# The mixers' first group in a one-core macaron block: where its loads, its first sums and the norms' squares stand

## The chip, the cores and the metric

The kernel runs on one core of a Trainium2 chip. The metric is the device time of one execution in microseconds (us), the median of several runs. Five engines work side by side, each through its own list of instructions in order, and wait for each other by semaphores: TensorE (PE, with its weight loads shown apart as PEld), VectorE (DVE), ScalarE (ACT), GpSimd (POOL) and SyncE (SP). SP, POOL and ACT also issue DMAs, each on a queue of its own.

## The reference

One block of a streaming encoder on 256 tokens of width 2048, all in float32: a half-step SwiGLU network, then attention and retention side by side on one wide projection, then a second half-step network and a last norm.

```python
x = x + 0.5 * swiglu_ffn(rmsnorm(x, norm_ffn1_g[l]), ...)
h = rmsnorm(x, norm_mix_g[l])
proj = h @ w_in[l]
q_a, k_a, v_a, q_r, k_r, v_r, g_r, gate_a, gate_r = jnp.split(proj, IN_SPLIT_POINTS, axis=-1)
...
x = x + merged @ w_out[l]
x = x + 0.5 * swiglu_ffn(rmsnorm(x, norm_ffn2_g[l]), ...)
return rmsnorm(x, norm_final_g)
```

`rmsnorm` multiplies a row by the reciprocal root of its mean square and by a gain per channel. The kernel multiplies by the gain ahead of the products and by the root (`rstd`) behind them.

## The kernel before

**Numbers in two halves.** Each float32 weight tile is split into a high part `hi`, a cast on ACT (L134), and a low part `lo`, a subtraction on DVE (L135). The left operands are split in the same way (L456, L457). A product is then three matmuls: high with high (L145), low left with high (L146), high left with low (L148). PE takes the weight's low part last, so `lo` may be ready a little later than `hi`.

**Entries.** The program is one list, `steps`, of entries. A standard entry multiplies two 128-row pieces of a 512-column block for both token halves, 12 matmuls; its weights come in one 512 KB tile `raw`, loaded by SP into a ring of five (`RAW_BUFS`). An entry of a `Strassen` group has 6 matmuls. A group computes two 512-column blocks at once by Strassen's scheme, over four weight pairs `k0`, `x0` to `k3`, `x3`, which POOL loads into act tiles (L552). Its first sum, `x += k` on DVE (L541, in `first`), gives the weights of the entries marked `s`; entries marked `r` use `k` alone. Groups are named by the entry at which they begin: `z390` is the mixers' first, `queries`. The low part of its entry `s` with pair 2 is `loz39002s`.

**What sets the order.** `run` (L254 on) goes through the entries. At entry c it first prepares entries up to c+3 (`prep_upto`: cast, subtraction, and what else `prep` does), then runs what `later(n, fn)` has put down for c, then issues c's matmuls. `load_some` lets a group's loads into the program from a given entry on, one an entry; for the first group of a `weave` that begins at eight entries ahead of the last one laid down (`first`, L722), for z390 at entry 382. In a group the first sum is part of `prep`, of the `r` entry of the same pair.

**The seam between the first network and the mixers.** Entries 376 to 383 are the last pass of the first network's down projection, four 512-column blocks of two entries each. When a block ends, `down_done` adds the product to x (L682, DVE, two pieces `xall`), and `done` of `x_updated` squares the new x with a row sum (L436, ACT, `nmsq`), at once, and three entries later calls `norm.put`: eight transposes on PE into two side banks (L468, `nmp`), four scalings on ACT out of these banks (L473, `nmx`), and the split `nma` (L456, L457). After the last square DVE adds up the sums and POOL takes the root (`tot` L442, `v` L382, `nmrstd` L383), and DVE makes `nmminus` from it (L445). There are two side banks. Entries 384 to 389 are the first six of the mixers' first projection, and at 390 z390 begins, woven with further standard entries (394, 399, 402). Four more operands of the norm (`nms5` to `nms7`, `nms3`) are made on DVE and ACT for the group's sums, from `nmf` (L494 to L503, L507, L508). The same `x_updated` stands between the mixers and the second network, with the norm `n2` and the group `z704`.

Of the kernel before, what the change touches and what calls it, by code (L numbers as in the profile page):

```python
# [18 lines left out]
D = 2048  # L19
# [7 lines left out]
NB = 512  # L27
# [7 lines left out]
EXTRA = 2  # L35
# [5 lines left out]
MIX_LEAD = 6  # L41
RET_WAIT = (14, 5)
HELD = 6
MIX_ADDED = (0,)
HEAD_AT = (3, 6, 10, 13, 17, 20, 24, 27)

MIX_SHARE = (0.5,) * 4 + (1.0,) * 4 + (0.0,) * 4 + (0.2,) * 4
SHARE = (0.75,) * 4 + (1.0,) * 4 + (0.0,) * 4 + (0.2,) * 4
ADDED = (0, 1)
ADD_WAIT = 6  # L50
# [30 lines left out]
def block_kernel(ctx: ExitStack, tc: tile.TileContext, x, g1, w1g, w1u, w1d, gm, w_in, rel, woa, wor, wo,  # L81
# [25 lines left out]
    steps = []  # L107
# [6 lines left out]
    def later(n, fn):  # L114
        due.setdefault(state["step"] + n, []).append(fn)
# [408 lines left out]
    class Strassen:  # L524
# [3 lines left out]

        def __init__(self, norm, w1, col1, w2, col2, evict, added=()):
            self.added, self.summed = added, set()  # L530
            self.add_wait = ADD_WAIT
            self.norm, self.w, self.col, self.evict = norm, (w1, w2), (col1, col2), evict
            self.x, self.kept, self.acc, self.wide = {}, {}, {}, {}
            self.name = f"z{len(steps)}"

        def rows(self, side, jc):
            j = KC * jc
            return ((2 * (j // 4) + side) * 4 + j % 4) * P

        def first(self, jc):  # L540
            nc.vector.tensor_add(self.x[jc], self.x[jc], self.kept[jc])  # L541
# [5 lines left out]
        def loads(self):  # L547


            def go(tiles, i, jc):  # L550
                tiles[jc] = apool.tile([P, KC, NB], F32, tag="act", name=f"{self.name}{'kx'[i]}{jc}")
                nc.gpsimd.dma_start(tiles[jc], chunk(self.w[i], self.rows(0, jc), self.col[i]))  # L552

            def add_on(jc):
                if jc not in self.summed:
                    self.summed.add(jc)
                    nc.gpsimd.dma_start(self.x[jc], self.kept[jc], accum_op=ALU.add)

            def second(jc):
                go(self.x, 1, jc)  # L560
                if jc in self.added:
                    later(self.add_wait, lambda: add_on(jc))

            return [
                (lambda jc=jc: second(jc)) if i else (lambda jc=jc: go(self.kept, 0, jc))
                for jc in range(HALF_K // KC) for i in range(2)
            ]
# [12 lines left out]
        def step(self, phase, jc, of_sum):  # L580
            made = {}
            name = f"{self.name}{phase}{jc}{'rs'[of_sum]}"
            n = HALF_K // KC

            def load():
                made["raw"] = weights_tile(f"raw{name}")
                i = 2 - phase
                fetch(made["raw"], self.w[i], self.rows(1, jc), self.col[i])

            def third():  # L590

                x, k = self.x[jc], self.kept[jc]
                nc.vector.tensor_sub(k, x, k)
                nc.gpsimd.dma_start(x, chunk(self.w[0], self.rows(1, jc), self.col[0]), accum_op=ALU.add)

            def prep():
                x = self.x[jc]
                if not of_sum:
                    if phase == 0:
                        made["w"] = split(self.kept[jc], name)  # L600
                        if jc not in self.added:
                            self.summed.add(jc)
                            self.first(jc)
                        return
                    raw = made.pop("raw")
                    made["w"] = split(raw, name)
                    if phase == 1:
                        nc.vector.tensor_add(x, x, raw)
                elif phase == 2:
                    made["w"] = split(self.kept.pop(jc), name)  # L610
                elif phase == 3:
                    made["w"] = split(self.x.pop(jc), name)
                else:
                    if phase == 0 and jc not in self.summed:
                        self.summed.add(jc)
                        self.first(jc)
                    made["w"] = split(x, name)
                    if phase == 1:
                        third()

            bank, form, fresh, closing = {
# [4 lines left out]
            }[phase, of_sum]  # L626

            def products():
                hi, lo = made["w"]
                if fresh and jc == 0:  # L630
                    self.bank(bank)
                three([
                    (
                        self.acc[bank], self.norm.form(form, KC * jc + i), (hi[:, i, :], lo[:, i, :]),
                        fresh and jc == 0 and i == 0, closing and jc == n - 1 and i == KC - 1,
                    )
                    for i in range(KC)
                ], True)
                if jc == n - 1:
                    self.end(phase, of_sum)  # L640

            loaded = not of_sum and phase in (1, 2)
            frees = ["raw"] if loaded else ["kept"] if of_sum and phase > 1 else []
            return Step(self, 0, load if loaded else None, prep, frees, products)

        def end(self, phase, of_sum):
# [41 lines left out]
    def x_updated(norm):  # L688


        def done(b):
            for t in range(NT):
                norm.square(b, t)
            later(3, lambda: norm.put(b))

        return done

    def weave(jobs, apart, groups, lead, share, start=None, extra=0):


        queue = [(job, k) for job in jobs for k in range(0, job.nk, KC)]
        at_hand = {}

        def next_standard():

            if len(queue) <= apart:
                return False
            job, k = queue[0]
            if any(at_hand.get(b, len(steps) + 1) > len(steps) for b in job.needs):
                return False  # L710
            steps.append(standard(job, k))
            del queue[0]
            if job.makes is not None and k + KC == job.nk:
                at_hand[job.makes] = len(steps) + 9
            return True

        for _ in range(lead):
            next_standard()
        seconds = []
        rate = (len(queue) - apart) / (len(groups) * sum(share))  # L720
        credit = 0.0
        first = max(len(steps) - 8, D // NB)  # L722
        for n, (b, make) in enumerate(groups.items()):
            group = make()
            group.added = group.added[:n]
            loads = group.loads()
            if start is not None and n == 0:
                loads[0] = lambda load=loads[0]: [start(), load()]
            kept.extend((first + i if n == 0 else 0, fn) for i, fn in enumerate(loads))
            for i, part in enumerate(group.steps()):  # L730
                if i == HALF_K // KC + 2:
                    seconds.append(len(steps))
                steps.extend(part)
                credit += rate * share[i]
                if i + 1 == len(share):
                    at_hand[b] = len(steps) + 7

                turn = i + 1 == 3 * (HALF_K // KC)
                if (turn or credit >= (0.2 if (i + 1) % (HALF_K // KC) == 0 else 0.6)) and next_standard():
                    credit -= 1  # L740
        if extra:
            due.setdefault(seconds[0], []).append(lambda: room.update(kept=room["kept"] + extra))
            due.setdefault(len(steps), []).append(lambda: room.update(kept=room["kept"] - extra))
        for job, k in queue:
            steps.append(standard(job, k))
# [332 lines left out]
    def gates(col1, col2, func, dsts):  # L1078
# [9 lines left out]

        return Strassen(nm, w_in0, col1, w_in0, col2, evict, MIX_ADDED)

    both = ("acc", "acc")
    groups = {
        b: (lambda b=b: gates(GA + b * NB, GG + b * NB, AF.Sigmoid, merge_dram[b])) for b in range(D // NB)
    }
    groups["gr"] = lambda: gates(GR, GR + NB, AF.Silu, ret_dram)

    def queries():
# [9 lines left out]

        return Strassen(nm, w_in0, QA, w_in0, QA + NB, evict, MIX_ADDED)

    groups = {"qa": queries, **groups}  # L1110
# [1 line left out]
        [proj(KA + b * NB, att_qk_done("ka", b), both) for b in range(2)]  # L1112
        + [proj(VA + b * NB, nat_done("va", b, AF.Copy), both) for b in range(2)]
        + [proj(VR + b * NB, nat_done("vr", b, AF.Copy), both) for b in range(2)],
        0, groups, MIX_LEAD, MIX_SHARE, None, EXTRA,
    )
    mixed = len(steps)
    for b in range(2):
# [210 lines left out]
```

## Time and profile before

| | us |
|---|---|
| median of 3 runs (2051.78 to 2052.53) | 2052.51 |
| profiled execution: its own time | 2052.5 |
| profiled execution: span from first to last instruction | 2050.7 |
| PE busy | 2033.1 |
| DVE busy | 1789.2 |
| ACT busy | 1499.5 |
| POOL busy | 343.8 |

The page gives busy time, then 40 slices of the span, the DMA queues and the chain of work that ended last. Matmuls overlap in this count: one is listed at 0.39 us, but the next starts 0.23 us behind it, so a PE that waits for 0.15 us still looks busy. Delays on PE are better read in the order of time, from one start to the next. The seam above lies at 640 to 765 us of the span. A row of the timeline has start, length, engine, line, operation, what is written and read, and in brackets the idle time of the engine before it with what ended that. Queue q0 of the DMA tables is POOL's, q1 is SP's.

### The profile page before, as it was taken

To read this page: it belongs to the slowest core of one execution; us is meant where nothing else is said; L and a number is where in the kernel's file an instruction comes from. 1 tells how busy PE (TensorE), PEld (TensorE's weight loads), DVE (VectorE), ACT (ScalarE), POOL (GpSimd) and SP (SyncE) were. 2 spreads that over 40 slices of the span, in tenths; PEclk is the share of its full clock that TensorE was granted. 3 is DMA by queue.
4 is the path that set the end of the run, shared out by engine and by line. 5 is a ranking of instruction groups with operands and counts; after the bars stand their busy time and mean duration, and the time that the engine had idled before them with its cause. 6 is when DMAs were issued, how large, how long until landed. Compare 5 with 4: busy or idle time off the path is not lost.

```text
span 2050.7 us, 26315 instructions
## 1 busy us (share of the span) xinstructions
PE 2033.1 (99%) x9188; PEld 1678.2 (82%) x9188; DVE 1789.2 (87%) x1837; ACT 1499.5 (73%) x1890; POOL 343.8 (17%) x403
## 2 busy tenths in 40 slices
PE   9999999999999999999999999999999999999998
PEld 7788888888888878888888888888788888888886
DVE  7999999999998799999987667569989999989996
ACT  7788888878787767777775434556788788888785
POOL 1221122212112022112120000011212221112200
PEclk9999999999999999999999999999999999999999
DMA  8888889988878679899896645576989988889974
GB/s 289 246 249 259 253 269 283 260 243 246 262 233 270 223 214 300 280 280 286 251 324 221 222 139 190 185 241 187 271 263 270 275 245 234 268 258 269 277 205 134
DMA packets 226853, 506.33 MB, mean 247 GB/s; under 512 B 15824, under 2 KB 16576, under 8 KB 226720
## 3 DMA queue, kind: packets, MB, share of 16 engines
q1 hardware_dynamic: 154560, 297.31, 43.1%
q0 software_dynamic: 67952, 198.36, 37.0%
q10 hardware_dynamic: 4208, 8.99, 1.2%
q8 instruction: 72, 1.18, 0.2%
q14 instruction: 61, 0.50, 0.1%
HBM read 472.08 MB, written 12.06 MB: 236 GB/s over the span
## 4 chain that ended last, share of the span: by engine, by line
PE 93%; DVE 3%; DMA 2%; ACT 1%; issue 1%; POOL 0%; SPq 0%; DVEq 0%; POOLq 0%; ACTq 0%
PE acc L148 15%; PE acc L145 15%; PE acc L146 15%; DMA z1030k<-in_ffn_w_up_dram 1%; DMA raw<-in_ffn_w_gate_dram 1%; DMA z1030x<-z1030k 1%; DVE lo L135 1%; PE z425a L145 0%; PE z777a L145 0%; PE z704a L146 0%; PE z958a L145 0%; PE z262a L145 0%; PE z190a L145 0%; PE z425a L146 0%; PE z226a L146 0%
## 5 line engine op out<-in xcount | busy, mean ns | idle before, releaser
L135 DVE TENSOR_TENSOR lo<-raw,hi 128x1024 fp32r<-128x1024 f32 x351 | 427.0, 1219 | 118.0 <-ACT hi L134 115.2
L134 ACT CAST hi<-raw 128x1024 fp32r<-128x1024 f32 x351 | 367.7, 1050 | 161.0 <-PE acc L146 125.7
L817 ACT ACTIVATE xall<-acc 128x512 f32<-128x512 f32 x160 | 94.5, 590 | 13.6 <-PE acc L148 9.7
L814 ACT ACTIVATE acc<-xall 128x512 f32<-128x512 f32 x160 | 95.9, 599 | 2.5
L145 PE MATMUL acc<-hi,mgh 128*128 128x512 f32 x128 | 50.2, 392 | 0.0
L146 PE MATMUL acc<-hi,mgl 128*128 128x512 f32 x128 | 49.8, 389 | 0.0
L148 PE MATMUL acc<-lo,mgh 128*128 128x512 f32 x128 | 35.5, 389 | 0.0
L145 PE MATMUL acc<-hi,nma01h 128*128 128x512 f32 x80 | 32.5, 407 | 0.0
L145 PE MATMUL acc<-hi,nma00h 128*128 128x512 f32 x80 | 32.3, 404 | 0.0
L146 PE MATMUL acc<-hi,nma01l 128*128 128x512 f32 x80 | 31.3, 391 | 0.0
L146 PE MATMUL acc<-hi,nma11l 128*128 128x512 f32 x80 | 31.3, 391 | 0.0
L146 PE MATMUL acc<-hi,nma00l 128*128 128x512 f32 x80 | 31.2, 390 | 0.0
L145 PE MATMUL acc<-hi,nma11h 128*128 128x512 f32 x80 | 31.2, 390 | 0.0
L146 PE MATMUL acc<-hi,nma10l 128*128 128x512 f32 x80 | 31.2, 390 | 0.0
L145 PE MATMUL acc<-hi,nma10h 128*128 128x512 f32 x80 | 31.2, 390 | 0.0
L148 PEld LDWEIGHTS acc<-lo,mgh 128*128 128x128 f32 x128 | 24.0, 188 | 5.0
L145 PEld LDWEIGHTS acc<-hi,mgh 128*128 128x128 f32 x128 | 24.0, 188 | 4.9
L146 PEld LDWEIGHTS acc<-hi,mgl 128*128 128x128 f32 x128 | 24.0, 188 | 4.8
L145 PE MATMUL acc<-hi,atth 128*128 128x512 f32 x64 | 26.2, 410 | 0.0
L148 PE MATMUL acc<-lo,nma01h 128*128 128x512 f32 x80 | 24.9, 393 | 0.6 <-DVE lo L135 0.6
L145 PE MATMUL acc<-hi,reth 128*128 128x512 f32 x64 | 25.3, 395 | 0.0
L146 PE MATMUL acc<-hi,attl 128*128 128x512 f32 x64 | 25.1, 392 | 0.0
(6884 smaller groups left out, 7258.8 us busy)
## 6 DMA issues: line engine op xcount, KB each, us to landing
raw<-in_ffn_w_down_dram SPq DMA_DIRECT2D x176, 512.0 KB, 6.7
raw<-in_w_in_dram SPq DMA_DIRECT2D x80, 512.0 KB, 5.0
raw<-in_w_out_dram SPq DMA_DIRECT2D x32, 512.0 KB, 4.1
raw<-in_ffn_w_up_dram SPq DMA_DIRECT2D x16, 512.0 KB, 5.0
raw<-in_w_out_att_dram SPq DMA_DIRECT2D x16, 512.0 KB, 4.3
raw<-in_w_out_ret_dram SPq DMA_DIRECT2D x16, 512.0 KB, 3.9
raw<-in_ffn_w_gate_dram SPq DMA_DIRECT2D x15, 512.0 KB, 4.9
z390x<-in_w_in_dram POOLq DMA_DIRECT2D x8, 512.0 KB, 8.7
```

Of the source, the lines that this page charges most:

```text
L134: nc.scalar.copy(hi, raw)
L135: nc.vector.tensor_sub(lo, raw, hi.bitcast(F32))
L145: nc.tensor.matmul(acc, ahi, whi, start=first, stop=False, **more)
L146: nc.tensor.matmul(acc, alo, whi, start=False, stop=False, **more)
L148: nc.tensor.matmul(acc, ahi, wlo, start=False, stop=last, **more)
L814: nc.scalar.activation(acc, xs[t][:, cols], AF.Copy, scale=2.0)
L817: nc.scalar.activation(xs[t][:, cols], acc, AF.Copy, scale=0.5)
```

## The change

Four things are changed, and no arithmetic.

1. `weave` takes `ahead` (8 if not given), and the mixers give `MIX_AHEAD`, 12: the loads of z390 may enter the program from entry 378 instead of 382, one an entry as before.
2. For that group alone (`early`), the first sum is no longer part of `prep`. It is put down with `later(FIRST_WAIT, ...)`, four entries behind the load of its x.
3. `first_once` replaces three places that tested and marked `summed`; it does the same.
4. In `x_updated`, for the norms nm and n2, the squares are put down with `later(1, ...)`, one entry behind, in place of at once. The transposes stay three entries behind.

```diff
+MIX_AHEAD = 12
+FIRST_WAIT = 4
...
-            self.add_wait = ADD_WAIT
+            self.add_wait, self.early = ADD_WAIT, False
...
+        def first_once(self, jc):
+            if jc not in self.summed:
+                self.summed.add(jc)
+                self.first(jc)
...
                 if jc in self.added:
                     later(self.add_wait, lambda: add_on(jc))
+                elif self.early:
+                    later(FIRST_WAIT, lambda: self.first_once(jc))
...
-                        if jc not in self.added:
-                            self.summed.add(jc)
-                            self.first(jc)
+                        if jc not in self.added and not self.early:
+                            self.first_once(jc)
...
-                    if phase == 0 and jc not in self.summed:
-                        self.summed.add(jc)
-                        self.first(jc)
+                    if phase == 0:
+                        self.first_once(jc)
...
             for t in range(NT):
-                norm.square(b, t)
+                later(1, lambda t=t: norm.square(b, t))
             later(3, lambda: norm.put(b))
...
-    def weave(jobs, apart, groups, lead, share, start=None, extra=0):
+    def weave(jobs, apart, groups, lead, share, start=None, extra=0, ahead=8):
...
-        first = max(len(steps) - 8, D // NB)
+        first = max(len(steps) - ahead, D // NB)
         for n, (b, make) in enumerate(groups.items()):
             group = make()
-            group.added = group.added[:n]
+            group.added, group.early = group.added[:n], n == 0 and ahead > 8
...
-        0, groups, MIX_LEAD, MIX_SHARE, None, EXTRA,
+        0, groups, MIX_LEAD, MIX_SHARE, None, EXTRA, MIX_AHEAD,
```

**POOL.** The rows stand between the last use of the bias table (`rel_ext`) and the group's later loads; the digit behind `z390k` or `z390x` is the pair. Before:

```order
L346 DMA rel_ext_86<-rel6_5743 128x2x384
L552 DMA z390k0_6096<-in_w_in_dram 128x2x512
L552 DMA z390x0_6141<-in_w_in_dram 128x2x512
L383 TENSOR_TENSOR nmrstd_91<-v_6173,mhalf_84 128x2
L552 DMA z390k1_6176<-in_w_in_dram 128x2x512
L552 DMA z390x1_6218<-in_w_in_dram 128x2x512
L552 DMA z390k2_6239<-in_w_in_dram 128x2x512
L552 DMA z390x2_6282<-in_w_in_dram 128x2x512
L552 DMA z390k3_6303<-in_w_in_dram 128x2x512
L552 DMA z390x3_6323<-in_w_in_dram 128x2x512
```

Of the changed kernel, at the same place on POOL:

```order
L348 DMA rel_ext_86<-rel6_5743 128x2x384
L559 DMA z390k0_5981<-in_w_in_dram 128x2x512
L559 DMA z390x0_6007<-in_w_in_dram 128x2x512
L559 DMA z390k1_6029<-in_w_in_dram 128x2x512
L559 DMA z390x1_6078<-in_w_in_dram 128x2x512
L559 DMA z390k2_6100<-in_w_in_dram 128x2x512
L559 DMA z390x2_6149<-in_w_in_dram 128x2x512
L559 DMA z390k3_6176<-in_w_in_dram 128x2x512
L385 TENSOR_TENSOR nmrstd_91<-v_6209,mhalf_84 128x2
L559 DMA z390x3_6226<-in_w_in_dram 128x2x512
```

Five loads have moved from behind the root `nmrstd` to ahead of it; two stood ahead of it already, and one stays behind.

**ACT.** The rows go from the scaling of the norm's block 1 (`nmx1`) to that of block 2 (`nmx2`); `hi386` is the cast for entry 386, and the digits in `nmp10` are block and side bank. Before:

```order
L473 ACTIVATE nmx1_6104<-nmp10_6105,gains_79 128x256 x2
L473 ACTIVATE nmx1_6104<-nmp11_6112,gains_79 128x256 x2
L456 CAST nma01h_6119<-nmx1_6104 128x512
L456 CAST nma11h_6123<-nmx1_6104 128x512
L134 CAST hi386_6143<-raw386_5989 128x1024
L436 ACTIVATE nmsq_6167,nmss_90<-xall_77 128x512
L436 ACTIVATE nmsq_6169,nmss_90<-xall_77 128x512
L134 CAST hi387_6178<-raw387_6009 128x1024
L473 ACTIVATE nmx2_6184<-nmp20_6185,gains_79 128x256 x2
```

Of the changed kernel, on ACT, between the same scalings:

```order
L475 ACTIVATE nmx1_6108<-nmp10_6109,gains_79 128x256 x2
L475 ACTIVATE nmx1_6108<-nmp11_6116,gains_79 128x256 x2
L458 CAST nma01h_6123<-nmx1_6108 128x512
L458 CAST nma11h_6127<-nmx1_6108 128x512
L438 ACTIVATE nmsq_6131,nmss_90<-xall_77 128x512
L438 ACTIVATE nmsq_6133,nmss_90<-xall_77 128x512
L136 CAST hi386_6151<-raw386_5987 128x1024
L136 CAST hi387_6178<-raw387_6013 128x1024
L475 ACTIVATE nmx2_6184<-nmp20_6185,gains_79 128x256 x2
```

The squares that stand here are those of block 2 now (of block 3 before); those of block 3 have moved to behind `nmx2` and its two casts. At the other norm, n2, the squares move in the same way past one cast `hi`, and one load of z704 of eight comes to stand ahead of `n2rstd` on POOL.

**DVE.** The rows begin with the low part of entry 386 and go to that of 389; `z390x0 <- z390x0, z390k0` is the first sum of pair 0. Before:

```order
L135 TENSOR_TENSOR lo386_6144<-raw386_5989,hi386_6143 128x1024
L494 TENSOR_TENSOR nmf0_6149<-nmx1_6104,nmx0_6035 128x4x128
L682 SCALAR_TENSOR_TENSOR xall_77<-acc85_0_6127,xall_77 128x512
L682 SCALAR_TENSOR_TENSOR xall_77<-acc85_1_6128,xall_77 128x512
L442 TENSOR_REDUCE tot_6171<-nmss_90 128x2
L382 TENSOR_SCALAR v_6173<-tot_6171 128x2
L135 TENSOR_TENSOR lo387_6179<-raw387_6009,hi387_6178 128x1024
L457 TENSOR_TENSOR nma00l_6051<-nmx2_6184,nma00h_6050 128x512
L457 TENSOR_TENSOR nma10l_6055<-nmx2_6184,nma10h_6054 128x512
L445 TENSOR_SCALAR nmminus_92<-nmrstd_91 128x2
L135 TENSOR_TENSOR lo388_6221<-raw388_6033,hi388_6220 128x1024
L135 TENSOR_TENSOR lo389_6242<-raw389_6076,hi389_6241 128x1024
```

Of the changed kernel, on DVE, from the same subtraction on (`lo389` is the row behind the last):

```order
L137 TENSOR_TENSOR lo386_6152<-raw386_5987,hi386_6151 128x1024
L548 TENSOR_TENSOR z390x0_6007<-z390x0_6007,z390k0_5981 128x1024
L496 TENSOR_TENSOR nmf0_6158<-nmx1_6108,nmx0_6037 128x4x128
L689 SCALAR_TENSOR_TENSOR xall_77<-acc85_0_6135,xall_77 128x512
L689 SCALAR_TENSOR_TENSOR xall_77<-acc85_1_6136,xall_77 128x512
L137 TENSOR_TENSOR lo387_6179<-raw387_6013,hi387_6178 128x1024
L459 TENSOR_TENSOR nma00l_6053<-nmx2_6184,nma00h_6052 128x512
L459 TENSOR_TENSOR nma10l_6057<-nmx2_6184,nma10h_6056 128x512
L444 TENSOR_REDUCE tot_6207<-nmss_90 128x2
L384 TENSOR_SCALAR v_6209<-tot_6207 128x2
L137 TENSOR_TENSOR lo388_6229<-raw388_6035,hi388_6228 128x1024
L548 TENSOR_TENSOR z390x1_6078<-z390x1_6078,z390k1_6029 128x1024
```

Two first sums, of pairs 0 and 1, have come in ahead of the group's own entries, and `tot` and `v` stand behind `lo387` and the two `nma` parts. The sum of pair 2 now stands where that of pair 0 stood, right behind `loz39000r`, and that of pair 3 behind `loz39000s`, four rows ahead of `lo394`; all four still stand ahead of `loz39002s`. The order of PE and of SP is the same in both kernels.

## The prediction

> **What bounds the kernel now.** The page's first part comes first, then PE in the order of time around the seam.
>
> ```profile
> PE 2033.1 (99%) x9188; PEld 1678.2 (82%) x9188; DVE 1789.2 (87%) x1837; ACT 1499.5 (73%) x1890; POOL 343.8 (17%) x403
> ```
>
> PE is busy for 99% of the span, so the change can only win where PE is late at the seam. Its timeline there:
>
> ```profile
> 692.46 1.04 PE L468 MATMUL nmp<-id_sb,xall 128*128 128x128 f32 x8
> 693.25 0.48 PE L145 MATMUL acc<-hi,nma00h 128*128 128x512 f32 x1
> ...
> 698.34 0.61 PE L148 MATMUL acc<-lo,nma10h 128*128 128x512 f32 x2
> 699.33 1.39 PE L468 MATMUL nmp<-id_sb,xall 128*128 128x128 f32 x8 [0.38 <-ACT nmx L473]
> 700.47 0.48 PE L145 MATMUL acc<-hi,nma01h 128*128 128x512 f32 x1
> ...
> 718.49 0.39 PE L146 MATMUL acc<-hi,nma11l 128*128 128x512 f32 x1
> 719.45 0.72 PE L148 MATMUL acc<-lo,nma01h 128*128 128x512 f32 x2 [0.58 <-DVE lo L135]
> ...
> 722.54 0.39 PE L146 MATMUL z390a<-hiz39003r,nma00l 128*128 128x512 f32 x1
> 722.92 0.74 PE L148 MATMUL z390a<-loz39003r,nma00h 128*128 128x512 f32 x2
> ...
> 724.21 0.39 PE L146 MATMUL z390c<-hiz39002s,nms5l 128*128 128x512 f32 x1
> 726.40 0.74 PE L148 MATMUL z390c<-loz39002s,nms5h 128*128 128x512 f32 x2 [1.80 <-DVE loz39002s L135]
> 726.98 0.40 PE L145 MATMUL z390c<-hiz39003s,nms5h 128*128 128x512 f32 x1
> ```
>
> Undisturbed, a matmul starts 0.23 us behind the last, and eight transposes take 0.79 us (692.46 to 693.25). From 698.34 to 700.47 stand two matmuls and eight transposes: 2.13 us for 0.45 + 0.79, so **0.89** lost, to the scaling `nmx` of block 2, which holds the side banks. Then `lo394` costs 719.45 - 718.49 - 0.23 = **0.73**, `loz39003r` 722.92 - 722.54 - 0.23 = **0.15**, and `loz39002s` 726.40 - 724.21 - 0.23 = **1.96**. Behind a wait the second matmul is late too: 726.98 is 0.58 behind two matmuls that need 0.45, a crumb of 0.13, and I count three of these, 0.35. The sum is **4.08 us**, and it is all that this seam can give up to 727 us. What makes the low parts late is DVE; the window over it (busy us of PE, PEld, DVE, ACT, POOL, then clock, DMA share, GB/s):
>
> ```profile
> 710.00:720.00 10.00, 9.42 (x42) 7.49 (x41) 10.00 (x12) 7.12 (x9) 0.00 (x0) 1.00 0.31 113
> ```
>
> DVE has no gap here, at full PE clock. It would be earlier only if it had begun earlier or had less to do. Ahead of 707 it does have gaps:
>
> ```profile
> 693.81 1.23 DVE L135 TENSOR_TENSOR lo<-raw,hi 128x1024 fp32r<-128x1024 f32 x1 [0.18 <-ACT hi L134]
> ...
> 697.64 0.16 DVE L442 TENSOR_REDUCE tot<-nmss 128x2 f32<-128x8 f32 x1 [0.81 <-ACT nmsq L436]
> ...
> 698.58 1.23 DVE L135 TENSOR_TENSOR lo<-raw,hi 128x1024 fp32r<-128x1024 f32 x1 [0.58 <-ACT hi L134]
> 700.69 0.69 DVE L457 TENSOR_TENSOR nma00l<-nmx,nma00h 128x512 fp32r<-128x512 f32 x1 [0.88 <-ACT nma00h L456]
> ...
> 703.63 1.22 DVE L135 TENSOR_TENSOR lo<-raw,hi 128x1024 fp32r<-128x1024 f32 x1 [0.25 <-ACT hi L134]
> ...
> 708.35 1.22 DVE L541 TENSOR_TENSOR z390x<-z390x,z390k 128x1024 f32<-128x1024 f32 x1
> ...
> 725.13 1.22 DVE L135 TENSOR_TENSOR loz39002s<-z390x,hiz39002s 128x1024 fp32r<-128x1024 f32 x1
> ```
>
> 0.81 + 0.58 + 0.88 + 0.25 = 2.52 us, each ended by ACT. ACT is late because it waits in the squares for DVE's new x:
>
> ```profile
> 680.01 0.63 ACT L436 ACTIVATE nmsq<-xall 128x512 f32<-128x512 f32 x1 [2.12 <-DVE xall L682]
> ...
> 681.40 1.04 ACT L134 CAST hi<-raw 128x1024 fp32r<-128x1024 f32 x1
> 682.34 1.56 ACT L473 ACTIVATE nmx<-nmp,gains 128x256 f32<-128x256 f32 x4
> ...
> 687.91 0.63 ACT L436 ACTIVATE nmsq<-xall 128x512 f32<-128x512 f32 x1 [1.89 <-DVE xall L682]
> ...
> 690.10 1.55 ACT L473 ACTIVATE nmx<-nmp,gains 128x256 f32<-128x256 f32 x4
> ...
> 692.73 1.04 ACT L134 CAST hi<-raw 128x1024 fp32r<-128x1024 f32 x1
> 696.27 0.64 ACT L436 ACTIVATE nmsq<-xall 128x512 f32<-128x512 f32 x1 [2.50 <-DVE xall L682]
> ...
> 698.45 1.55 ACT L473 ACTIVATE nmx<-nmp,gains 128x256 f32<-128x256 f32 x4
> ```
>
> So the chain is: squares wait for x, casts and scalings wait behind the squares, DVE behind these, and PE behind DVE.
>
> **Squares one entry behind, norm nm.** One block of ACT's work without the wait is 690.10 - 682.34 - 1.89 = 5.87 us, and 698.45 - 690.10 - 2.50 = 5.85 us. What is late next is the tile of entry 383, whose cast `hi383` (the 681.40 row) stands ahead of the first scaling. I work out below that it lands at 681.0. Then the scalings begin at 681.0 + 1.05 = 682.05, 687.9 and 693.8, the last 4.7 us earlier than now. PE wants the side banks at 698.34 + 0.45 = 698.8, the scaling ends at 695.4, and the 0.89 goes. Between the second scaling and `hi386` lay 692.73 - 690.10 = 2.63 us; the two squares now stand there too, 1.28, so `hi386` is at 691.8 and `lo386` at 691.8 + 1.08 = 692.87, **0.94** earlier than 693.81. On DVE the first two sums fill what were gaps, and the 2.52 go as well: `nmx` of block 2, for which it waited at 700.69, is there 4.7 us earlier, and `tot` stands behind three more rows. The price is the root: with `tot` behind `lo387` and two `nma` parts it comes at about 700 instead of 698.10. Only the load of `x3` and the evictions of the first projection wait behind it.
>
> **Sums ahead.** No instruction is added or dropped: four sums before, four after, at 1.22 us (708.35). All four stand ahead of `loz39002s` in both, so it gains 0.94 + 2.52 = 3.46 and ends at 725.13 + 1.22 - 3.46 = **722.89**. PE would want it at 724.44 less the stalls removed ahead of it (0.89, 0.73, 0.15, two crumbs), 722.4. It is still 0.45 late, and that remains. `lo394` had three sums ahead and now has four, so it gains only 3.46 - 1.14 (a sum's start to the next row); it wants 0.73 + 0.89, and has 2.32. **4.08 - 0.45 = 3.6 us.**
>
> A sum in its new place waits for its loads on DVE, with every low part queued behind it and PE behind those. The loads:
>
> ```profile
> 659.14 0.73 POOL L552 DMA_DIRECT2D z390x<-in_w_in_dram  x1
> ...
> 698.10 0.72 POOL L383 TENSOR_TENSOR nmrstd<-v,mhalf 128x2 f32<-128x2 f32 x1 [38.22 <-DVE v L382]
> ```
>
> ```profile
> z390x<-in_w_in_dram POOLq DMA_DIRECT2D x1, 512.0 KB, 11.3
> DMA packets 1462, 4.01 MB, mean 401 GB/s; under 512 B 133, under 2 KB 197, under 8 KB 1462
> ```
>
> `x0` lands at 659.14 + 11.3 = 670.4 and its sum now stands at 694: 23 us of room. `x3` alone is left behind the root, issued at about 701 and wanted at about 711 (its sum stands right behind `loz39000s`, which ended at 713.5 with one sum fewer ahead: 713.5 - 3.46 + 1.14), 10 us against its neighbours' 11.3 under contention that five moved loads no longer make. I take it as in time: nothing.
>
> **Loads ahead.** POOL idles for 38.22 us, so its five issues (0.73 each) cost nothing on POOL; their bytes meet SP's. The queues while both had work (662 to 666 us: packets, MB, share), and the tile of entry 383:
>
> ```profile
> q0 software_dynamic: 301, 1.05, 64.9%
> q1 hardware_dynamic: 305, 0.59, 38.2%
> ```
>
> ```profile
> 668.26 0.37 SPq L125 DMA_DIRECT2D raw<-in_ffn_w_down_dram  x1
> ```
>
> ```profile
> raw<-in_ffn_w_down_dram SPq DMA_DIRECT2D x1, 512.0 KB, 6.1
> ```
>
> It landed at 674.4. From 670.4 SP was alone: 4.0 us at 0.40 MB/us (the 401 GB/s) is 1.6 MB still to come. Five tiles are 2.6 MB, at 1.05 / 4 = 0.26 MB/us ten us more of contention, to 680.5. In that time SP gets 0.59 / 4 = 0.15 MB/us, and its 1.6 MB need 10.7 us: **681.0**. The bounds are equal shares, 1.6 / 0.20 = 8 us and 678.4, and the longest landing of the stretch from 640 to 760 us:
>
> ```profile
> rawz42510r<-in_w_in_dram SPq DMA_DIRECT2D x1, 512.0 KB, 18.7
> ```
>
> That would be 668.26 + 18.7 = 687.0. I take the shares measured nearest in place and kind. [...]
>
> **n2.** The same edit, and one load of z704 earlier.
>
> ```profile
> 1365.89 0.69 POOL L383 TENSOR_TENSOR n2rstd<-v,mhalf 128x2 f32<-128x2 f32 x1 [141.75 <-DVE v L382]
> ```
>
> PE shows no wait from 1290 to 1380 us, so nothing can be won; the root is some 0.3 us later behind one cast, the other loads by as much. The cover is PE's queue of prepared entries; if it is gone, it costs those 0.3 us. I take **nothing**. `first_once` only regroups code: nothing.
>
> Against the profiled execution, 2052.5 us and equal to the median (2052.51), the sum gives 2052.5 - 3.6 = **2048.9**.
>
> **The rivals.** *A: the tile is not late.* With equal shares it lands at 678.4, and `hi383` waits only for the matmuls that free its buffer.
>
> ```profile
> 679.09 0.39 PE L146 MATMUL acc<-hi,f1a9l 128*128 128x512 f32 x1
> ```
>
> Freed at 679.5, the chain is up to 1 us earlier (not 1.5, since PE's own transposes of block 1 come next), the 0.45 is gone, and all 4.08 go, with a crumb or two behind 727: 2048.2. [...]
>
> *B: DVE stays the bound.* If the tile lands 2 to 3 us later than 681, or one gap of 0.9 and more stays on DVE (`lo387` or `nma` waiting for ACT, which has 5.9 us of work a block, and PE's block of two entries and eight transposes is 24 x 0.23 + 0.79 = 6.3), 1 to 2 us come of it: 2051.
>
> *C, the other side: SP starves.* Every us by which the tile is later than 681.0 moves scalings, casts and `loz39002s` by a us. From 684.5 on, 3.46 later, the change loses. At the 687.0 of the longest row `loz39002s` ends at 728.9 instead of 726.35, and the time is 2055.0. For it: SP's share falls to 36% of the bytes with seven tiles queued against it. Against: it needs a tile 16.2 us in flight, and the longest one in this place, POOL's own, took 11.3.
>
> *D: it does not do what it says.* ACT may wait in the squares one place later as long as now, because DVE's new x has come behind a sum: the square of block 3 is reached at about 696.4, when x is ready at 697. That is 0.6 instead of 2.50, and little hangs on it. If all the waits only moved like this, 2052.5.
>
> **How the numbers follow.** Forecast 2048.9: 0.50; A 2048.2: 0.22; B 2051: 0.14; C 2055: 0.07; D 2052.5: 0.07. The range runs from 2047.4 (A with 0.8 of later crumbs) to 2052.8 (D, and 0.3 for the spread between runs) and leaves out C and a tail below. A measurement of this kernel can tell 0.2%, 4.1 us, from no change: 2048.4 and 2056.6 are the borders. Nearly all of A, and a little of the forecast, lies under the lower one, 0.26; C beyond 688.5 above the upper one, 0.04; the rest, 0.70, lies within.
>
> **What would show it.** Right: the tile of entry 383 lands near 681; no wait of ACT in `nmsq` over 1 us; transposes at 698.8 without a bracket; DVE without gaps from `lo386` on; `loz39002s` ends near 722.9 and PE waits 0.4 for it; DMA rates drop around 700 and rise around 672. Wrong: a bracket on DVE's sums naming a DMA (loads late), PE stalls at entries 380 to 389 naming `hi` or `lo` (C), or a stall at the second seam near 1370.

## The result and the profile after

| | before | after |
|---|---|---|
| median, us | 2052.58 (14 runs, 2051.18 to 2053.80) | 2048.31 (14 runs, 2047.02 to 2050.28) |
| ratio | | 0.9981, 95% interval 0.9974 to 0.9988 |
| span of the profiled execution | 2050.7 | 2046.5 |
| PE busy | 2033.1 | 2031.7 |

The changed kernel is faster by 4.3 us, 0.19%, clear of no change. The interval allows a gain of 2.5 to 5.3 us. The forecast was 2048.9, the range 2047.4 to 2052.8.

A caution ahead of all comparisons. Two executions are not at the same place when they reach the seam. PE's first matmul of L302 (L304 in the changed kernel) behind 600 us stands ahead of everything that the change touches, and I use it as a **mark**:

```profile
651.34 0.23 PE L302 MATMUL gps<-id_sb,grows 16*128 16x16 f32 x1
```

```profile
650.72 0.23 PE L304 MATMUL gps<-id_sb,grows 16*128 16x16 f32 x1
```

The first row is of before, the second of after. In the other profiles below it lies between 650.66 and 652.07, whatever the kernel. So 0.62 us of the 4.2 between the two spans is spread. Where two kernels are compared, times behind the mark are used.

PE's timeline of after, at the two places that cost most before:

```profile
697.73 0.63 PE L150 MATMUL acc<-lo,nma10h 128*128 128x512 f32 x2
698.19 1.04 PE L470 MATMUL nmp<-id_sb,xall 128*128 128x128 f32 x8
698.98 0.48 PE L147 MATMUL acc<-hi,nma01h 128*128 128x512 f32 x1
...
721.52 0.39 PE L148 MATMUL z390c<-hiz39002s,nms5l 128*128 128x512 f32 x1
722.39 0.74 PE L150 MATMUL z390c<-loz39002s,nms5h 128*128 128x512 f32 x2 [0.48 <-DVE loz39002s L137]
```

The transposes of block 3 start 0.46 behind two matmuls and take 0.79: nothing is lost there. `lo394` and `loz39003r` cost nothing. Only `loz39002s` is late, by 722.39 - 721.52 - 0.23 = 0.64. That matmul came at 726.40 before and at 722.39 now, 4.01 earlier, and without the mark's 0.62 the seam gives **3.4 us**.

ACT's waits from 660 to 710 us by what ended them (sum, times, longest), of before and then of after:

```profile
ACT nmsq L436 <- DVE xall L682: 8.6, 5, 2.5
```

```profile
ACT hi L136 <- DMA raw<-in_ffn_w_down_dram: 6.1, 3, 2.7
```

The wait in the squares is gone. In its place ACT waits for DMAs, which it never did here before: for the three tiles ahead of the scalings. ACT's timeline of after:

```profile
681.22 1.05 ACT L136 CAST hi<-raw 128x1024 fp32r<-128x1024 f32 x1 [2.68 <-DMA raw<-in_ffn_w_down_dram]
682.18 1.56 ACT L475 ACTIVATE nmx<-nmp,gains 128x256 f32<-128x256 f32 x4
...
687.94 1.55 ACT L475 ACTIVATE nmx<-nmp,gains 128x256 f32<-128x256 f32 x4
...
693.70 1.55 ACT L475 ACTIVATE nmx<-nmp,gains 128x256 f32<-128x256 f32 x4
```

DVE's timeline of after, with the first and last rows of the stretch:

```profile
692.88 1.22 DVE L137 TENSOR_TENSOR lo<-raw,hi 128x1024 fp32r<-128x1024 f32 x1 [1.00 <-ACT hi L136]
694.02 1.22 DVE L548 TENSOR_TENSOR z390x<-z390x,z390k 128x1024 f32<-128x1024 f32 x1
...
721.11 1.23 DVE L137 TENSOR_TENSOR loz39002s<-z390x,hiz39002s 128x1024 fp32r<-128x1024 f32 x1
```

Between them DVE never waits. `lo386` is 42.16 behind the mark (42.47 before) and `loz39002s` ends 71.62 behind it (75.0 before). So the chain begins only 0.31 earlier; the rest of the 3.4 comes from the stretch itself, in which the gaps have closed.

### The profile page after: what moved, and what is told of

Read it like the earlier page. It is cut to its first block, busy times and chain, and to the rows that moved or that the text cites. A ratio compares the mean times of both kernels' runs of the same rounds, so it can differ in the third digit from the quotient of the medians.

```text
span 2046.5 us, 26320 instructions
## 1 busy us (share of the span) xinstructions
PE 2031.7 (99%) x9188; PEld 1678.3 (82%) x9188; DVE 1788.5 (87%) x1837; ACT 1499.2 (73%) x1890; POOL 344.8 (17%) x403
## 4 chain that ended last, share of the span: by engine, by line
PE 94%; DVE 2%; DMA 2%; issue 1%; ACT 0%; POOL 0%; DVEq 0%; POOLq 0%; ACTq 0%
PE acc L150 15%; PE acc L147 15%; PE acc L148 15%; DMA z1030k<-in_ffn_w_up_dram 1%; DMA z1030x<-z1030k 1%; DVE lo L137 0%; DMA raw<-in_ffn_w_gate_dram 0%; PE z704a L150 0%; PE z425a L147 0%; PE z922a L147 0%; PE z885a L148 0%; PE z226a L147 0%; PE z190a L147 0%; PE z46a L147 0%; PE z262a L148 0%
## 5 line engine op out<-in xcount | busy, mean ns | idle before, releaser
L824 ACT ACTIVATE xall<-acc 128x512 f32<-128x512 f32 x160 | 94.5, 590 | 13.5 <-PE acc L150 9.7
L148 PE MATMUL acc<-hi,retl 128*128 128x512 f32 x64 | 24.9, 389 | 0.0
```

Of the source, the lines that this page charges most:

```text
L148: nc.tensor.matmul(acc, alo, whi, start=False, stop=False, **more)
L824: nc.scalar.activation(xs[t][:, cols], acc, AF.Copy, scale=0.5)
```

## The experiments

Ten runs were made: eight other kernels, and the changed kernel and one of the eight a second time. "Late starts" is one sum over PE's timeline from 690 to 730 us: a matmul's start minus that of the one ahead of it minus 0.227 (0.105 between transposes), where 0.09 or more is left. "Tile" is the landing of the tile of entry 383 behind the mark. "Wait" is the part of the late starts at the first matmul with `loz39002s`. All three are worked out from the timelines.

| run | what it has of the change | median, us | before, same chip | ratio, 95% interval | late starts | tile | wait |
|---|---|---|---|---|---|---|---|
| before | nothing | 2052.58 | | | 4.06 | 23.0 | 1.96 |
| after | all | 2048.31 | 2052.58 | 0.9974 to 0.9988 | 0.95 | 30.4 | 0.65 |
| sq_only | squares | 2048.22 | 2052.57 | 0.9972 to 0.9989 | 0.51 | 24.5 | 0.30 |
| loads_only | loads | 2054.11 | 2052.40 | 0.9996 to 1.0015 | 5.09 | 28.8 | 1.98 |
| loads_sums | loads, sums | 2053.21 | 2052.57 | 0.9996 to 1.0014 | 4.61 | 28.5 | 0 |
| sums_late | loads, squares | 2049.56 | 2052.57 | 0.9977 to 0.9994 | 0.91 | 30.0 | 0.69 |
| n2_undone | all but n2 | 2048.08 | 2052.57 | 0.9971 to 0.9989 | 0 | 29.6 | 0 |
| a13w5 | all, one load more ahead | 2049.51 | 2052.40 | 0.9976 to 0.9995 | 0.74 | 30.3 | 0.52 |
| a11w3 | all, one load fewer ahead | 2047.48 | 2052.40 | 0.9964 to 0.9984 | 0 | 28.3 | 0 |
| a11w2 | as a11w3, sums an entry earlier | 2047.69 | 2052.40 | 0.9968 to 0.9988 | 0.09 | 27.8 | 0 |
| change_again | all | 2048.86 | 2053.23 | 0.9974 to 0.9992 | 0.22 | 29.8 | 0 |
| a11w3_again | as a11w3 | 2047.24 | 2053.23 | 0.9965 to 0.9985 | 0 | 29.0 | 0 |

**Squares alone (sq_only).**

```diff
-MIX_AHEAD = 12
+MIX_AHEAD = 8
```

> Part 4 alone: squares one entry behind, loads and first sums as before (the order then has one load more ahead of the root, k1). The measure is PE's late starts from 690 to 730 us (start to start, beyond the undisturbed pitch): 4.0 us before, 0.8 with the whole change. My theory: ACT's waits go, so DVE's gaps shrink, but two sums more stand between the cast of 386 and loz39002s and five loads still come behind a later root, so 1.5 to 2.9 us of late starts stay, 2050 to 2051. Rival 1, the squares do all: 0.8 left, 2048.3. Rival 2, loads and sums do all: 4.0 left, 2052.5.

The first rival came true: 2048.22, as fast as the whole change. My reckoning had a slip, since no sums are added between the cast of 386 and `loz39002s`: all four stand there in both kernels. ACT and DVE of this run:

```profile
678.89 1.06 ACT L136 CAST hi<-raw 128x1024 fp32r<-128x1024 f32 x1 [1.67 <-PE acc L148]
679.85 1.56 ACT L475 ACTIVATE nmx<-nmp,gains 128x256 f32<-128x256 f32 x4
```

```profile
691.08 1.23 DVE L137 TENSOR_TENSOR lo<-raw,hi 128x1024 fp32r<-128x1024 f32 x1 [1.41 <-ACT hi L136]
...
697.42 1.23 DVE L137 TENSOR_TENSOR lo<-raw,hi 128x1024 fp32r<-128x1024 f32 x1 [0.57 <-ACT hi L136]
...
720.71 1.21 DVE L137 TENSOR_TENSOR loz39002s<-z390x,hiz39002s 128x1024 fp32r<-128x1024 f32 x1
```

Here the cast of 383 waits for PE, not for its tile, and `lo386` is 40.42 behind the mark, 1.7 earlier than with the whole change. From `lo386` to `loz39002s` DVE takes 29.63 (31.32 before) against 28.23 with the whole change, since it waits for ACT a little again. With the whole change DVE thus begins 1.7 later and is 1.4 quicker on the way, and PE's wait differs by 0.35 only: parts 1 and 2 cancel in the changed kernel. The 1.4 are not all due to the early sums. In `sums_late`, described below, the loads are moved and the sums are not:

```profile
693.01 1.23 DVE L137 TENSOR_TENSOR lo<-raw,hi 128x1024 fp32r<-128x1024 f32 x1 [0.99 <-ACT hi L136]
...
721.73 1.22 DVE L137 TENSOR_TENSOR loz39002s<-z390x,hiz39002s 128x1024 fp32r<-128x1024 f32 x1
```

There it takes 28.72. So 0.9 of the 1.4 goes because a DVE that begins later waits less for ACT, and the early sums take off the last 0.5.

**Loads alone, and loads with sums.** Both have the squares at once:

```diff
-                later(1, lambda t=t: norm.square(b, t))
+                norm.square(b, t)
```

and `loads_only` also has the first sums in `prep`:

```diff
-            group.added, group.early = group.added[:n], n == 0 and ahead > 8
+            group.added, group.early = group.added[:n], False
```

> Part 1 alone: loads from entry 378, first sums and squares as before. My theory: the loads by themselves move nothing that ends last. The tile of entry 383 lands near 680 to 681, about when its cast is reached behind the squares anyway (681.4), so the late starts stay at 3.7 to 4.7 us and the time at 2052.2 to 2053. Rival: the later tile delays casts that the squares had not, more than 1 us is lost, 2053.5 or more; or the group's tiles had been late before, and 1 us or more is won.

The loads by themselves do harm: late starts grew by 1.0, 0.4 beyond my upper end, and the median lies where the rival that delays casts had it, though its interval doesn't part it from before. I had looked at one tile only. ACT's timeline of this run:

```profile
678.02 1.05 ACT L136 CAST hi<-raw 128x1024 fp32r<-128x1024 f32 x1 [1.32 <-DMA raw<-in_ffn_w_down_dram]
681.01 0.63 ACT L438 ACTIVATE nmsq<-xall 128x512 f32<-128x512 f32 x1 [1.95 <-DVE xall L689]
...
683.20 1.56 ACT L475 ACTIVATE nmx<-nmp,gains 128x256 f32<-128x256 f32 x4
```

The cast of entry 382 waits for its tile as well, and the squares' waits still follow. The first scaling begins 32.1 behind this run's mark (683.20 - 651.11), where before had 31.0 (682.34 - 651.34).

> Parts 1 and 2 alone: loads from entry 378 and first sums four entries behind them, squares at once as before. My theory: ACT still waits in the squares, and the first sum, ahead of DVE's new x, makes that wait 1.1 us longer, so the transposes of block 3 wait 1.5 to 2 us instead of 0.8, and what the sums win behind them is given back: 3.0 to 4.5 us of late starts stay, 2051.5 to 2053. Rival 2, loads and sums do all: 0.8 left, 2048.3. Rival 1, they do nothing: 4.0 left, 2052.5, with the transposes' wait unchanged at 0.8.

The direction is as expected, the sizes lie just beyond the upper ends: 4.61 of late starts, and 2053.21. ACT waits longer in the squares of block 3 because the first sum stands ahead of DVE's new x:

```profile
698.39 0.63 ACT L438 ACTIVATE nmsq<-xall 128x512 f32<-128x512 f32 x1 [3.63 <-DVE xall L689]
```

It was 2.50 before. PE's transposes then wait 2.45, 0.45 more than I gave, and something follows that I had not expected, on which more at the end. The wait for `loz39002s` is gone in this run, but only because PE comes 4.5 us later. **Without the squares' move, the other two parts win nothing.**

**Loads and squares, sums in `prep` (sums_late).**

> The whole change but for part 2: loads from entry 378 and squares one entry behind, first sums in the group's own preparation as before. My theory: the early sums fill DVE's gaps while it waits for ACT, of which about 1.6 us of the 2.3 would be there without them; so 0.65 us more stay than with the whole change: 1.2 to 1.8 of late starts, 2048.8 to 2049.3. Rival: the sums carry the gain, and without them over 3 us stay, 2051.5 or more. Other rival: they add nothing, 0.8 left.

The median of 2049.56 is 0.3 above what I gave, 1.3 above sq_only; the late starts, 0.91, lie below it. Its tile landed 0.4 earlier than after's; if the wait follows the tile one to one, as is shown below, it would be 1.1 at the same landing against 0.65, so the early sums are worth about 0.45 on PE, as much as DVE's stretch is shorter by them (28.72 to 28.23) and near the 0.65 that I gave. In the medians, 1.25 apart with overlapping intervals, their size isn't settled.

**n2 (n2_undone).**

```diff
-                later(1, lambda t=t: norm.square(b, t))
+                later(1, lambda t=t: norm.square(b, t)) if norm is nm else norm.square(b, t)
```

> The whole change, but the squares of n2 stand at once as before. Between the profiles of before and after a PE wait at z740's loz74002r, some 1450 us in, went from 0.77 to 0.41 us. My theory: the n2 part does nothing for the time: at the first seam 0.8 us of late starts as with the change, and 2048.3 within 0.5. If the n2 part makes the 0.36, the wait is back at 0.77 and the time 2048.7; if it costs something, 2047.9 or less. Whether the 0.77 is back tells it, not the time.

The time is the same, 2048.08. PE's lateness for the low parts of z740, from start to start, was 0.6 to 1.2 us in the four profiles with n2's squares at once and 0.1 to 1.2 in the eight with them an entry later: a spread in which no effect of n2 can be told.

This run brought an answer I hadn't asked for. At the first seam it is the changed kernel, yet its wait for `loz39002s` is 0, not 0.65. Its cast of 383, `lo` and PE:

```profile
680.45 1.05 ACT L136 CAST hi<-raw 128x1024 fp32r<-128x1024 f32 x1 [2.23 <-DMA raw<-in_ffn_w_down_dram]
```

```profile
720.33 1.22 DVE L137 TENSOR_TENSOR loz39002s<-z390x,hiz39002s 128x1024 fp32r<-128x1024 f32 x1
```

```profile
721.80 0.62 PE L150 MATMUL z390c<-loz39002s,nms5h 128*128 128x512 f32 x2
```

The tile came 0.8 earlier (29.6 against 30.4 behind the mark), and so did the end of `loz39002s` (70.8 against 71.6), 0.25 ahead of PE. One tile seemed to set what was left.

**More and less contention (a13w5, a11w3, a11w2).** The sums keep their places in the first two; in the third they are an entry earlier.

```diff
-MIX_AHEAD = 12
-FIRST_WAIT = 4
+MIX_AHEAD = 13
+FIRST_WAIT = 5
```

> The whole change with one more load ahead of the root: loads from entry 377, first sums five entries behind theirs, so the sums stand where the change has them and x3 is the eighth tile that POOL queues before 666 us. My theory: the tile of entry 383 sets the start of ACT's and DVE's chain, one to one. It shares the DMA engines with one tile more (2.1 us of POOL's at the rate of the changed kernel's landings) and lands at 682.5 to 683.3, loz39002s comes 2 us later, and 1.9 to 2.9 us of late starts stay from 690 to 730 us; 2049.5 to 2050.5. Rival: what is left is DVE's own work; then the wait stays at 0 to 0.8 and the time at 2048.3.

This failed: the tile was not later (30.3), and the wait fell with it, by 0.13 for 0.12. In after POOL's seven tiles ahead of the root were through at 680.93, and SP's tile landed at 681.12, 0.2 behind the seventh. Here it landed at 681.87, 0.3 behind the seventh (681.56) and ahead of the eighth (683.95), so the longer queue added nothing to it. The wait did follow the tile, but the edit didn't move the tile as I had said.

> The whole change with one tile fewer ahead of the root: loads from entry 379, sums three entries behind, at the places of the change. My theory: the tile of entry 383 lands at 678.5 to 679.2, when the buffer of its cast comes free; ACT's chain is 1.5 to 2 us earlier than with the change, PE waits for loz39002s not at all, late starts 0 to 0.2 from 690 to 730 us; 2047.5 to 2048.3. Rival: k3 and x3 behind the root land too late for the sum of pair 3, DVE waits for a DMA, and the 0.8 or more stay.

With `MIX_AHEAD = 11` and `FIRST_WAIT = 3` POOL ends a tile earlier, and SP's tile lands 28.3 behind the mark, 2.1 earlier, as forecast. No low part is late up to 735 us, and DVE names no DMA. The median is the lowest of all but one.

> As the run with loads from entry 379, but with the sums two entries behind their loads, one entry earlier on DVE, each in or next to a gap in which DVE waits for ACT. My theory: the tile in time and the sums in gaps together leave no wait for a low part up to 730 us and take some of the crumbs behind (0.1 each at 725, 732, 742 and 747 us): 2047.2 to 2048.0, the best of these, though by less than the time can tell. Rival: the sum of pair 3, now ahead of loz39000s, waits on DVE for x3, which stands behind the root: a bracket naming a DMA, and 0.5 us or more on PE.

DVE did wait for x3, as the rival said, but for less than PE's margin:

```profile
709.49 1.22 DVE L548 TENSOR_TENSOR z390x<-z390x,z390k 128x1024 f32<-128x1024 f32 x1 [0.95 <-DMA z390x<-in_w_in_dram]
```

PE lost nothing up to 730 us. It is not better than a11w3.

**The changed kernel and a11w3 again, on one chip.**

> The changed kernel once more, to see how much of its one wait on PE is its own and how much is the landing of one tile. From PE's first instruction at L304 behind 600 us the tile of entry 383 landed 30.4 us later in the changed kernel's profile (wait for loz39002s 0.65), 30.3 in the run with one load more (0.52), 29.6 where the squares of n2 were undone (0). My theory: it lies again between 29.5 and 30.5, and the wait follows it one to one: landing minus 29.75, nothing below that. Rival: the wait has another cause and does not follow; then a landing near 30.4 goes with no wait, or one near 29.6 with 0.6.

The tile landed 29.8 behind the mark, and there is no wait beyond a crumb, as the rule (landing minus 29.75) says. Over six profiles with these places of the sums, tiles at 30.4, 30.3, 29.8, 29.6, 29.0 and 28.3 go with waits of 0.65, 0.52, 0, 0, 0 and 0. The way from the one to the other is fixed: `lo386` begins 11.75 to 11.77 behind the landing in all of these but a11w3 (12.14, where PE's transposes hold the second scaling), and `loz39002s` 28.24 behind `lo386` in all six. What the changed kernel loses at `loz39002s` is the spread of one transfer's landing.

> The kernel with loads from entry 379 and sums three entries behind, beside the changed kernel on the same chip. My theory: the tile at 28 to 28.6 us behind the same mark, no wait for a low part from 690 to 735 us, and 0.3 to 1.0 us less than the changed kernel. Rival: the 0.8 us between their medians so far (2048.31 and 2047.48, on two chips' runs) is spread of the measurement, and the two lie within 0.3 us.

No wait again, the tile a little later than I gave (29.0). The median is 1.6 us under the changed kernel's beside it, as 0.8 before; but the intervals overlap, and the two profiled spans are 2045.2 and 2045.1. The late starts end at 730 us and tell 0.2 to 1.0 of it. Followed on to PE's first matmul of the next group, z425, some 770 us in, a11w3's two profiles have it 118.23 and 118.55 behind the mark, the changed kernel's two 120.00 and 119.49, n2_undone (the changed kernel up to there) 119.11, sq_only 119.59 and before 123.34. At this seam a11w3 was thus 0.6 to 1.8 ahead of the changed kernel, and 1.0 to 1.4 ahead of the squares alone, in every profile. Further on the profiles differ by as much again for other reasons (z740 above). That a11w3's whole time is shorter than the changed kernel's is likely, not shown; that it is faster than before is shown twice (0.9964 to 0.9984 and 0.9965 to 0.9985).

## Why the prediction was right

It was right in its chain: squares wait for x, casts and scalings behind the squares, DVE behind these, PE behind DVE. Its size was near, in part by luck. The median of 2048.31 lies nearer to rival A's 2048.2 than to the forecast's 2048.9, though A's condition, a tile in time, did not hold; the interval holds both. Of the 4.2 us between the two spans 0.62 lies ahead of the mark. To PE's first matmul of z425 the gain behind the mark is 3.3 and 3.9 in the changed kernel's two profiles and 4.2 in n2_undone.

- *Four stalls, 4.08 in all.* Three are gone as forecast. The fourth was to keep 0.45 and kept 0.65, or 0 in the other two profiles, change_again and n2_undone. Counted by late starts the seam gave 4.06 - 0.95 = 3.1 in the profiled pair (3.4 by the matmul of `loz39002s`), and 3.8 and 4.1 in those two (4.06 - 0.22, 4.06 - 0), against 3.6.
- *Squares.* No wait of ACT in `nmsq` is left. The scalings were forecast at 682.05, 687.9 and 693.8 and came at 682.18, 687.94 and 693.70; `lo386` at 692.87 and came at 692.88. This is luck: counted from the mark everything was some 0.6 later than I had it. DVE began only 0.31 earlier, not 0.94, and its way to `loz39002s` became 3.09 shorter (31.32 to 28.23), not 2.52, so two errors of 0.6 cancelled. The four gaps that I counted were each some 0.08 longer than their brackets, since rows that don't wait begin that much ahead of the last one's end (707.21 + 1.23 and 708.35 in before), and one of 0.19 at `nmminus` I left out.
- *Loads.* The tile of entry 383 was forecast at 681.0 from the two queues' shares, and landed 30.4 behind the mark, which is 681.7 on before's clock:

```profile
667.65 0.37 SPq L127 DMA_DIRECT2D raw<-in_ffn_w_down_dram  x1
```

```profile
raw<-in_ffn_w_down_dram SPq DMA_DIRECT2D x1, 512.0 KB, 13.5
```

  Over 671 to 680 us of after the queues moved

```profile
q0 software_dynamic: 569, 2.05, 59.6%
q1 hardware_dynamic: 741, 1.42, 43.9%
```

  0.23 and 0.16 MB/us, against the 0.26 and 0.15 taken from before. The shares stayed unequal, so rival A's even halves (678.4) didn't come; nor were the packets here nearly equal in number (569 and 741), as they were in the row of the prediction (301 and 305). A's end of the sum was reached all the same where the tile landed under a microsecond earlier. Rival C needed a tile 16.2 us in flight; this tile took 13.5 in after and 12.9 in change_again.
- *Sums, root, n2.* The sum of pair 0 waited for nothing at 694.02, the root came at 699.74 and x3 was loaded at 701.36, landing at 707.1 for a sum at 711.22. n2 gave nothing that can be told.
- *What the prediction did not see* is that its gain needs only one of the parts. It took the parts as one chain, with the late tile as a bound of the squares' move. The runs show that the late tile is a cost of the moved loads: `lo386` begins 41.72 (sums_late) and 42.15 (after) behind the mark with them, against 40.42 with the squares alone. At `loz39002s` 0.4 of this is left in sums_late (70.44 against 70.05), or 0.8 if its tile had landed when after's did. The early sums return 0.5 there, and the squares alone bring as much as the whole change. With one load fewer ahead DVE begins about as early as with the squares alone, at 40.41 and 40.75 in a11w3's two profiles, and with the early sums it is at `loz39002s` by 1.4 and 1.1 sooner.

## What to carry to other kernels

Move first the instruction that waits at the head of an in-order engine for another engine's result (here ACT's squares, 8.6 us of waits before): one entry's delay of the squares freed casts and scalings behind them and was worth the whole change, while the work moved around it (loads, sums) exchanged one delay for another; with one load fewer moved the kernel stood 1.0 to 1.4 us ahead of the squares alone at this seam, in two profiles. When loads are begun earlier, look for the transfers of the other queue that they then meet (SP's tile of entry 383 took 6.1 us to land before and 13.5 in after), and ask what is queued behind the one that comes last. Before two profiles are compared by the microsecond, find a common instruction ahead of the change and count from there.

## What the runs showed of the hardware

PE was granted half its clock (0.50) for 3.41 us in one run. In loads_sums it waits 2.45 us ahead of the transposes of block 3, and the matmuls behind these stand 0.43 apart instead of 0.23, PE's timeline first:

```profile
701.45 1.53 PE L470 MATMUL nmp<-id_sb,xall 128*128 128x128 f32 x8 [2.45 <-ACT nmx L475]
702.63 0.77 PE L147 MATMUL acc<-hi,nma01h 128*128 128x512 f32 x1
703.21 0.63 PE L148 MATMUL acc<-hi,nma01l 128*128 128x512 f32 x1
703.63 0.63 PE L147 MATMUL acc<-hi,nma01h 128*128 128x512 f32 x1
```

The windows of the same run (the columns as above) give the granted clock, 0.50 from 702.54 to 705.95, and 1.00 ahead of it and behind:

```profile
699.13:702.54 3.41, 1.02 (x7) 0.79 (x8) 1.55 (x3) 3.38 (x8) 2.15 (x3) 1.00 0.11 18
702.54:705.95 3.41, 3.41 (x11) 2.73 (x10) 3.05 (x5) 3.41 (x6) 0.00 (x0) 0.50 0.96 353
706.00:710.00 4.00, 4.00 (x19) 3.30 (x19) 4.00 (x6) 3.97 (x8) 0.00 (x0) 1.00 0.82 248
```

In the 3.41 us just ahead, a stretch as long as that at 0.50, PE did nothing but wait and do transposes, 1.02 us of them. A wait of 1.80 us (before, at `loz39002s`) and one of 1.48 (loads_only, at the same transposes) had no such sequel: the clock granted was 1.00 from 726.40 to 730.00 of before, and in loads_only the matmuls behind the transposes stand 0.23 apart. Around the wait of 1.48 PE was busy for 1.90 of 3.41 us, with 1.00 granted:

```profile
698.77:702.18 3.41, 1.90 (x12) 1.53 (x13) 1.95 (x4) 3.38 (x8) 2.14 (x3) 1.00 0.30 76
```

What brought the half clock about, the wait of 2.45 us, the little work in the whole stretch ahead or something else, is not shown: it is one case. The wait itself cost PE 2.6 us and the half clock about 1.7 more, half of the 3.41.
